# Chunks of the gate modulation loaded two ahead, in chained groups of four products; input rows loaded a pair earlier; one column's weight sums a product later

## The chip, the cores and the metric

The kernel runs on one core of one Trainium2 chip. The metric is the device time of one execution in microseconds (us), as the median over several runs. A profile of one execution shows what each engine does: TensorE (PE, with its weight loads as PEld), VectorE (DVE), ScalarE (ACT), GpSimd (POOL), and SyncE (SP), which here only issues DMAs; SPq is its queue of issues.

## The reference

One encoder layer for two sequences (prompt and sample) of 1024 rows and 1024 features, in fp32. All weights are shared.

```python
mod = jax.nn.silu(c) @ w_ada + b_ada                       # c: (1, 1024), w_ada: (1024, 6 * 1024)
sh1, sc1, ga1, sh2, sc2, ga2 = jnp.split(mod, 6)
h = rmsnorm(x, g_mix) * (1 + sc1) + sh1
z = h @ w_in                                               # latents for attention, and f_in
mix = concat(mla_group(z...), fourier_group(f_in, w_four)) @ w_out
x = x + ga1 * mix
h2 = rmsnorm(x, g_ffn) * (1 + sc2) + sh2
x = x + ga2 * ((silu(h2 @ w_gate) * (h2 @ w_up)) @ w_down)
y = rmsnorm(x, g_final)
```

## The kernel before, in words

The kernel is written in a framework that traces the Python program, orders the instructions of each engine by priority and readiness, and puts in the semaphores. So the order on an engine isn't quite that of the code; `tc.issue_after(i)` makes what is traced inside it stand behind instruction `i` on the same engine, and `behind()` (line 70) does so for the last split's two instructions. Every engine, and SP's queue of DMAs, then takes its list strictly in order.

**Products in three.** Every large fp32 product is made of three PE passes (`mm3`, lines 77 to 80): each operand is split into a rounded part and a rest by one ACT cast (line 62) and one DVE subtraction (line 63).

**Stage 1** (lines 153 to 610) works on eight pairs of row tiles, `k` = 0 to 7 (four per sequence). For a pair, `x_load` (340) loads two tiles `xt` of 128 rows into four buffers; `norm` (346) squares them on ACT, takes the root on POOL (`rstd`, 94) and scales on DVE (357); `flip` (359) transposes them on PE (370), in four groups g of two column blocks; `zproj` (397) projects one tile onto the latents and writes `lat` from DVE (418, 419) behind a root on POOL; `latents` (427) transposes `lat` on PE (433), splits it and stores both parts to `lat_d` (438); `evenodd` and `fourier_in` (381, 440) make the Fourier input, 24 passes against `wcs` each. `zproj` also stores `kv` to `ckv_d` (424). While a pair is projected the next one is flipped.

**The gate modulation** runs as filler in stage 1. `extras` (265) is a generator that `first_pair` (546) and `pair` (563) call three times a pair. It has eight chunks c of `w_ada` for the gates ga1 and ga2; a chunk is 1 MB, loaded by `mod_load` (199) as two DMAs of 512 KB, one per gate, into one of two buffers `wada`, and multiplied by `mod_mm` (207) in four products of 32 rows by 512 columns, each into its own quarter of a PSUM bank. Column groups j = 0, 1 come from the first DMA and 2, 3 from the second. At a step, the next chunk is loaded and then the present one multiplied. After the chunks, the gates' row is written out (`mod_row`, 214) and the Fourier part of `w_out` is folded with the gates (293 to 306). The shift and scale modulation earlier on (lines 465 to 529) uses the same `mod_mm`.

**The FFN** (lines 1307 to 1484, `s` the sequence) is a Strassen-like scheme over half-size blocks: 22 columns n, each of seven products `step(0)` to `step(6)` of 12 passes, into three PSUM banks x, y, z that are accumulated into more than once. Between them DVE takes sums from a bank (`u2`, 1451; `u3`, 1457, by `add`, line 137), which frees that bank for the next product into it. The weights of a column are seven combinations of four raw blocks: `sums_w` (1214) makes four differences (line 134), and `hl` (1299) splits each into two buffers `wh`, `wl`, eight of each. While column n is multiplied, the weights of n+1 are split; the sums are POOL's, but DVE makes those of the first two columns. In the first column of the first sequence (`s == 0 and n == 0`, line 1405) the last input blocks H are still being split as well (`prep`, two steps at j < 3), and the last two row tiles are transposed (`flip2`, 1239).

Of the kernel before, what the change touches and what calls it, by code (L numbers as in the profile page):

```python
# [16 lines left out]
ALU = mybir.AluOpType  # L17
# [7 lines left out]
NC = D // P  # L25
# [27 lines left out]
def hybrid_encoder_kernel(ctx: ExitStack, tc: tile.TileContext, a: dict):  # L53
    nc = tc.nc

    here = {}
# [13 lines left out]
    def behind():  # L70

        st = ExitStack()
        st.enter_context(tc.issue_after(here["a"]))
        st.enter_context(tc.issue_after(here["v"]))
        return st
# [83 lines left out]
    with ExitStack() as st:  # L159
# [36 lines left out]
        def wada_tile():  # L196
            return w2.tile([P, 4, 512], F32, tag="wada", name="wada", bufs=2)

        def mod_load(c, cols, wt):
            for j, (lo_, n) in enumerate(cols):  # L200
                nj = n // 512
                nc.sync.dma_start(
                    wt[:, j * nj : (j + 1) * nj, :],
                    a["w_ada"][c * P : (c + 1) * P, lo_ : lo_ + n].rearrange("p (j n) -> p j n", n=512))
            return wt

        def mod_mm(key, c, wt):
            if c == 0:
                mods[key] = bank()
            for j in range(4):  # L210
                here["m"] = nc.tensor.matmul(
                    mods[key][32 * j : 32 * j + 32, :], scT[:, c, :], wt[:, j, :], start=(c == 0), stop=(c == NC - 1)).ins

        def mod_row(key):
            mr = stile("modrow")
# [49 lines left out]
        def extras():  # L265


            cols1 = [(2 * D, D), (5 * D, D)]
            wt = mod_load(0, cols1, wada_tile())
            yield  # L270
            yield
            wo4 = []
            for c in range(NC):
                if c + 1 < NC:
                    nxt = mod_load(c + 1, cols1, wada_tile())
                else:
                    wo4.append(wo_load(2, wada_tile().rearrange("p a b -> p (a b)").rearrange("p (a b) -> p a b", a=2)))
                    bga = stile("bga")
                    nc.sync.dma_start(bga, a["bga"])
                mod_mm(1, c, wt)  # L280
                wt = nxt
                yield
            small_weights()
            mr = mod_row(1)
            add(mr, mr, bga, nc.vector)
            nc.sync.dma_start(ga_d, mr)
            wo4.append(wo_load(3, wada_tile().rearrange("p a b -> p (a b)").rearrange("p (a b) -> p a b", a=2)))
            yield
            for g in range(2):
                gs = slice(512 * g, 512 * g + 512)  # L290
                ga = [w.tile([P, 512], F32, tag=f"gah{s}", name="gah") for s in range(2)]
                for s in range(2):
                    nc.sync.dma_start(ga[s], ga_d[32 * g + s, :].partition_broadcast(P))
                yield
                for c in range(4):
                    k, i = c // 2, c % 2
                    ps = bank()
                    for q in range(2):
                        nc.tensor.matmul(ps[64 * q : 64 * q + 64, :], lw[:, 2 * i + q, 64 * k : 64 * k + 64], wo4[i][:, q, gs],
                                         start=True, stop=True)  # L300
                    for s in range(2):
                        so = stile("so")
                        nc.vector.tensor_tensor(out=so, in0=ps, in1=ga[s], op=ALU.mult)
                        nc.sync.dma_start(wm_d[s][:, c, gs], so)
                        if k == 1:
                            nc.sync.dma_start(
                                wn_d[NNYQ * s : NNYQ * s + NNYQ, gs].rearrange("(k r) n -> r k n", k=3)[4 * i : 4 * i + 4],
                                so[0:97:32, :].unsqueeze(1).broadcast_to([4, 3, 512]))
                    if c % 2 == 1:
                        yield  # L310
            yield
# [28 lines left out]
        def x_load(k):  # L340
            s, j = pairs[k]
            st1["x", k] = [xtile() for _ in range(2)]
            for u in range(2):
                nc.sync.dma_start(st1["x", k][u], xs[s][rows(j, u), :])
# [193 lines left out]
        with behind():  # L538
            norm(1)
        norm1 = here["p"]  # L540
        zproj(0, 0)
        evenodd(0, norm1)
        nk = len(pairs)
        more = extras()

        def first_pair():
            zproj(0, 1)
            fourier_in(0, 0)
            with tc.issue_after(here["t"]):
                flip(1, 0)  # L550
                flip(1, 1)
            next(more, None)
            latents(0, 0)
            flip(1, 2)
            flip(1, 3)
            next(more, None)
            latents(0, 1)
            next(more, None)
            fourier_in(0, 1)
            norm(2)  # L560
            evenodd(1, here["p"])

        def pair(k):
            if k == 0:
                return first_pair()
            zproj(k, 0)
            if k + 1 < nk:
                flip(k + 1, 0)
                flip(k + 1, 1)
            next(more, None)  # L570
            zproj(k, 1)
            latents(k, 0)
            here["l0"] = here["a"], here["v"]
            if k + 1 < nk:
                flip(k + 1, 2)
                flip(k + 1, 3)
            if k + 2 < nk:
                x_load(k + 2)
            next(more, None)
            fourier_in(k, 0)  # L580
            latents(k, 1)
            next(more, None)
            fourier_in(k, 1)
            if k + 2 < nk:
                norm(k + 2)
            if k + 1 < nk:
                evenodd(k + 1, here["p"])
# [559 lines left out]
    with ExitStack() as st:  # L1147
# [66 lines left out]
        def sums_w(b, out, eng):  # L1214

            b11, b21, b12, b22 = b
            t3, t2, t4 = (out(i) for i in range(3))
            sub(t3, b22, b12, eng)
            sub(b12, b12, b11, eng)
            sub(t2, b22, b12, eng)  # L1220
            here["s"] = sub(t4, b21, t2, eng)
            return [b11, t2, b21, t3, b12, t4, b22]
# [73 lines left out]
        def val():  # L1296
            return w5.tile([P, 512], F32, tag="v", name="val", bufs=VALS)
# [13 lines left out]
        for s in range(2):  # L1311
# [80 lines left out]
            for n, f in enumerate(order):  # L1392
# [10 lines left out]
                def step(j, ps, k, first, src=src):  # L1403
                    prod(ps, k, cur[j], first)
                    if s == 0 and n == 0:
                        if j == 0:
                            cur.extend(hl(v) for v in w0[4:])
                            w0.clear()
                            S["n3"] = norm3(1, S.pop("jk3").bitcast(BF16))
                        if j < 3:  # L1410
                            with behind():
                                for _ in range(2):
                                    next(prep, None)
                            if j == 1:
                                with behind():
                                    S.pop("n3")()
                            return
                        if j == 3:
                            src = S["w1"] = sums_w(src, lambda i: val(), nc.vector)
                        src = S["w1"]  # L1420
                        for i in ((), (), (), (0, 1), (2, 3), (4,), (5, 6))[j]:
                            nxt.append(hl(src[i]))
                        if j == 6:
                            flip2(3, [S.pop(("xn", 1, 3, u)) for u in range(2)], bank, lambda g: val())
                    elif s == 1 and n == 0:
                        if j == 2:
                            with tc.issue_after(here["u2"]):
                                S["w1"] = sums_w(src, lambda i: val(), nc.vector)
                        with behind(), tc.issue_after(here["c"]) if j > 1 else ExitStack():
                            for i in ((), (), (0,), (1, 2), (3,), (4,), (5, 6))[j]:  # L1430
                                nxt.append(hl(S["w1"][i]))
                        if j == 6:
                            S.pop("w1")
                    elif src is not None:
                        nxt.append(hl(src[j]))
                    if s == 0 and n == 1 and j == 2:
                        S.pop("w1", None)
# [17 lines left out]
                pend()  # L1455
                step(3, y, 6, False)
                u3 = val()
                add(u3, y, p1, nc.vector)
                step(4, z, 4, True)
                add(u3, z, u3, nc.vector)  # L1460
                pend()
# [303 lines left out]
```

## Time and profile before

| | us |
|---|---|
| median of 3 runs | 2079.11 (2078.59 to 2080.59) |
| the profiled execution, its own time | 2073.8 |
| its span | 2072.0 |
| PE busy in the span | 2023.1 |
| stage 1 (to about) | 200 |
| FFN, first column starts | 769 |

The profile is one execution; its times count from the start of its span. Rows of the timeline give start, duration, engine, line, operation, output and inputs, and in brackets the idle time ahead of it and what ended that. An fp32 product of 32 x 512 shows as two records, so a chunk's four products are x8. Rows of the table by stretches give busy time of each engine (with its number of instructions), then the granted clock of PE, the busy share of the DMA engines and GB/s. "L12" is line 12 of the kernel. PE takes up nearly the whole span, so what counts is where PE waits.

### The profile page before, as it was taken

To read this page: it belongs to the slowest core of one execution; us is meant where nothing else is said; L and a number is where in the kernel's file an instruction comes from. 1 tells how busy PE (TensorE), PEld (TensorE's weight loads), DVE (VectorE), ACT (ScalarE), POOL (GpSimd) and SP (SyncE) were. 2 spreads that over 40 slices of the span, in tenths; PEclk is the share of its full clock that TensorE was granted. 3 is DMA by queue.
4 is the path that set the end of the run, shared out by engine and by line. 5 is a ranking of instruction groups with operands and counts; after the bars stand their busy time and mean duration, and the time that the engine had idled before them with its cause. 6 is when DMAs were issued, how large, how long until landed. Compare 5 with 4: busy or idle time off the path is not lost.

```text
span 2072.0 us, 28814 instructions
## 1 busy us (share of the span) xinstructions
PE 2023.1 (98%) x10044; PEld 1659.5 (80%) x10044; DVE 1414.3 (68%) x2085; ACT 901.7 (44%) x1763; POOL 820.4 (40%) x1013
## 2 busy tenths in 40 slices
PE   6899999999999999999999999999999999999998
PEld 3688878888888877888888888877788888888886
DVE  4557767666677679767677676778665666667685
ACT  3666535555565554332333355454223232336451
POOL 0555111111313317779778510334554454420142
PEclk9999999999999999999999999999999999999999
DMA  9675885544643465546446477675322222257662
GB/s 395 216 238 180 274 316 172 134 90 102 168 102 122 154 244 203 179 157 213 173 158 219 154 274 260 212 242 182 118 102 102 96 108 102 86 171 275 230 232 94
DMA packets 185342, 375.49 MB, mean 181 GB/s; under 512 B 18764, under 2 KB 58444, under 8 KB 182124
## 3 DMA queue, kind: packets, MB, share of 16 engines
q1 hardware_dynamic: 167212, 318.06, 45.1%
q0 software_dynamic: 17984, 55.59, 9.0%
q8 instruction: 79, 1.29, 0.3%
q14 instruction: 67, 0.55, 0.1%
HBM read 259.47 MB, written 122.49 MB: 184 GB/s over the span
## 4 chain that ended last, share of the span: by engine, by line
PE 51%; DVE 4%; DMA 3%; issue 1%; ACT 1%; POOL 1%; SPq 1%; DVEq 0%; ACTq 0%; POOLq 0%
PE bank L80 17%; PE bank L79 17%; PE bank L78 17%; DVE wl L63 2%; DMA draw<-s_d 1%; DVE val L137 1%; ACT wh L62 1%; DMA H<-s_d 1%; DMA val<-x_d 1%; POOL val L137 0%; DVE val L1571 0%; DMA H<-in_w_down_dram 0%; DMA X<-hc_d 0%; SPq L1531 0%; ACT H L62 0%
## 5 line engine op out<-in xcount | busy, mean ns | idle before, releaser
L80 PE MATMUL bank<-H,wl 128*128 128x512 f32 x1232 | 491.3, 399 | 0.2 <-DVE wl L63 0.2
L78 PE MATMUL bank<-H,wh 128*128 128x512 f32 x1232 | 483.7, 393 | 2.6 <-DVE val L137 1.0
L79 PE MATMUL bank<-H,wh 128*128 128x512 f32 x1232 | 485.6, 394 | 0.3 <-DVE H L63 0.3
L79 PEld LDWEIGHTS bank<-H,wh 128*128 128x128 f32 x1232 | 231.2, 188 | 60.5 <-DVE H L63 0.6
L78 PEld LDWEIGHTS bank<-H,wh 128*128 128x128 f32 x1232 | 231.3, 188 | 59.9 <-DVE val L137 1.8
L80 PEld LDWEIGHTS bank<-H,wl 128*128 128x128 f32 x1232 | 231.3, 188 | 53.6 <-DVE wl L63 0.5
L63 DVE TENSOR_TENSOR wl<-draw,wh 128x512 fp32r<-128x512 f32 x286 | 201.6, 739 | 85.3 <-ACT wh L62 84.7
L137 DVE TENSOR_TENSOR val<-bank,val 128x512 f32<-128x512 f32 x200 | 136.6, 689 | 159.6 <-PE bank L80 152.5
L62 ACT CAST wh<-draw 128x512 fp32r<-128x512 f32 x286 | 168.7, 619 | 160.6 <-PE bank L79 81.0
L137 POOL TENSOR_TENSOR val<-val 128x512 f32<-128x512 f32 x58 | 83.2, 1444 | 367.1 <-DVE val L1545 188.6
L79 PE MATMUL bank<-wl,wh 128*128 128x512 f32 x572 | 223.7, 391 | 2.5 <-DVE wl L63 2.5
L62 ACT CAST wh<-rgu 128x512 fp32r<-128x512 f32 x172 | 106.7, 620 | 271.8 <-PE bank L79 209.4
L78 PE MATMUL bank<-wh 128*128 128x512 f32 x572 | 222.6, 389 | 0.0
L80 PE MATMUL bank<-wh,wl 128*128 128x512 f32 x572 | 222.6, 389 | 0.0
L62 ACT CAST wh<-val 128x512 fp32r<-128x512 f32 x133 | 82.1, 620 | 269.1 <-PE bank L79 256.1
L63 DVE TENSOR_TENSOR wl<-val,wh 128x512 fp32r<-128x512 f32 x133 | 132.5, 998 | 76.0 <-ACT wh L62 76.0
L63 DVE TENSOR_TENSOR wl<-rgu,wh 128x512 fp32r<-128x512 f32 x172 | 168.7, 981 | 3.6 <-ACT wh L62 3.5
L134 POOL TENSOR_TENSOR val<-rgu 128x512 f32<-128x512 f32 x80 | 116.7, 1459 | 99.5 <-DMA rgu<-in_wgu_dram 95.7
L79 PEld LDWEIGHTS bank<-wl,wh 128*128 128x128 f32 x572 | 107.3, 188 | 27.7 <-DVE wl L63 5.8
L78 PEld LDWEIGHTS bank<-wh 128*128 128x128 f32 x572 | 107.4, 188 | 22.7
L80 PEld LDWEIGHTS bank<-wh,wl 128*128 128x128 f32 x572 | 107.4, 188 | 22.0
L1024 DVE TENSOR_REDUCE mx<-ps_s 128x1 f32<-128x1024 f32 x64 | 78.2, 1222 | 62.8 <-PE ps_s L1019 62.6
(356 smaller groups left out, 4120.1 us busy)
## 6 DMA issues: line engine op xcount, KB each, us to landing
rgu<-in_wgu_dram SPq DMA_DIRECT2D x86, 512.0 KB, 4.2
draw<-s_d SPq DMA_DIRECT2D x143, 256.0 KB, 3.9
s_d<-val POOLq DMA_DIRECT2D x88, 256.0 KB, 4.2
draw<-t_d SPq DMA_DIRECT2D x88, 256.0 KB, 4.5
s_d<-val SPq DMA_DIRECT2D x66, 256.0 KB, 3.3
draw<-in_w_down_dram SPq DMA_DIRECT2D x55, 256.0 KB, 4.6
wada<-in_w_ada_dram SPq DMA_DIRECT2D x11, 1024.0 KB, 7.2
xt<-in_x_dram SPq DMA_DIRECT2D x16, 512.0 KB, 6.4
```

Of the source, the lines that this page charges most:

```text
L62: here["a"] = nc.scalar.copy(hi, src).ins
L63: here["v"] = nc.vector.tensor_tensor(out=lo, in0=src, in1=rd(hi), op=ALU.subtract).ins
L78: nc.tensor.matmul(out, lh, rh, start=first, stop=False, skip_group_check=cont)
L79: nc.tensor.matmul(out, lh, rl, start=False, stop=False, skip_group_check=cont)
L80: here["t"] = nc.tensor.matmul(out, ll, rh, start=False, stop=last, skip_group_check=cont).ins
L134: return eng.tensor_tensor(out=out, in0=x, in1=y, op=ALU.subtract).ins
L137: eng.tensor_tensor(out=out, in0=x, in1=y, op=ALU.add)
L1024: nc.vector.tensor_reduce(out=mx, in_=ps, axis=AX.X, op=ALU.max)
```

## The change

It has four parts. In `mod_mm` the four products are taken in the order j = 2, 3, 0, 1, and each stands behind the one ahead of it. In `extras` two chunks are loaded at the first step, and at each later step the present chunk is multiplied first and then the chunk two ahead loaded; the first step is moved up ahead of `zproj(0, 0)` and there is no empty step, so that the first `mod_mm` comes two calls earlier. `x_load` is called for the pair three ahead instead of two, and once more in `first_pair`. In the FFN's first column the DVE sums for the second column move from step 3 to step 4, behind `u3`, and the splits that use them with them; two more steps of `prep` come at step 3.

```diff
-            for j in range(4):
-                here["m"] = nc.tensor.matmul(
-                    mods[key][32 * j : 32 * j + 32, :], scT[:, c, :], wt[:, j, :], start=(c == 0), stop=(c == NC - 1)).ins
+            for n, j in enumerate((2, 3, 0, 1)):
+                with tc.issue_after(here["m"]) if n else ExitStack():
+                    here["m"] = nc.tensor.matmul(
+                        mods[key][32 * j : 32 * j + 32, :], scT[:, c, :], wt[:, j, :], start=(c == 0), stop=(c == NC - 1)).ins
...
-            wt = mod_load(0, cols1, wada_tile())
-            yield
+            ahead = [mod_load(c, cols1, wada_tile()) for c in range(2)]
             yield
             wo4 = []
             for c in range(NC):
-                if c + 1 < NC:
-                    nxt = mod_load(c + 1, cols1, wada_tile())
-                else:
+                mod_mm(1, c, ahead.pop(0))
+                if c + 2 < NC:
+                    ahead.append(mod_load(c + 2, cols1, wada_tile()))
+                elif c + 2 == NC:
...
-                mod_mm(1, c, wt)
-                wt = nxt
                 yield
...
+        more = extras()
+        next(more)
         zproj(0, 0)
         evenodd(0, norm1)
         nk = len(pairs)
-        more = extras()
...
             flip(1, 2)
             flip(1, 3)
+            x_load(3)
...
-            if k + 2 < nk:
-                x_load(k + 2)
+            if k + 3 < nk:
+                x_load(k + 3)
...
-                        if j < 3:
-                            with behind():
+                        if j < 4:
+                            with behind() if j < 3 else ExitStack():
                                 for _ in range(2):
                                     next(prep, None)
...
-                        if j == 3:
-                            src = S["w1"] = sums_w(src, lambda i: val(), nc.vector)
+                        if j == 4:
+                            with tc.issue_after(here["u3"]):
+                                S["w1"] = sums_w(src, lambda i: val(), nc.vector)
                         src = S["w1"]
-                        for i in ((), (), (), (0, 1), (2, 3), (4,), (5, 6))[j]:
+                        for i in ((), (), (), (), (0, 1, 2), (3, 4), (5, 6))[j]:
...
-                add(u3, y, p1, nc.vector)
+                here["u3"] = nc.vector.tensor_tensor(out=u3, in0=y, in1=p1, op=ALU.add).ins
```

What it moves on the engines is shown at three places. First PE in the first pair, from the last pass of the even Fourier product to the first of the odd one (`xt` are the flips' transposes, `lat` the latents', `wada` the chunk's products). Before:

```order
L80 MATMUL bank<-wcs_h,eol 128x280
L370 MATMUL bank<-ident,xt 128x128 x8
L433 MATMUL bank<-ident,lat 128x128 x4
L370 MATMUL bank<-ident,xt 128x128 x8
L433 MATMUL bank<-ident,lat 128x128 x4
L211 MATMUL bank<-wada,scT 32x512 x4
L78 MATMUL bank<-wcs_h,eoh 128x256
```

and now:

```order
L80 MATMUL bank<-wcs_h,eol 128x280
L369 MATMUL bank<-ident,xt 128x128 x8
L212 MATMUL bank<-wada,scT 32x512 x4
L432 MATMUL bank<-ident,lat 128x128 x4
L369 MATMUL bank<-ident,xt 128x128 x8
L212 MATMUL bank<-wada,scT 32x512 x4
L432 MATMUL bank<-ident,lat 128x128 x4
L78 MATMUL bank<-wcs_h,eoh 128x256
```

The first two chunks' groups now stand ahead of the two transposes of latents instead of one group behind both. The third chunk's group stands between the 23rd and the 24th pass of the odd Fourier product, the fourth between the 6th and 7th pass of `zproj(1, 1)`; before, the second and third stood ahead of `zproj(1, 1)` and of `fourier_in(1, 0)`.

Second SP's queue of DMAs at the same place, from the loads of pair 2 on; each `wada` number is one chunk, its x2 the two halves. Before:

```order
L344 DMA xt_456<-in_x0_dram 128x1024
L424 DMA ckv_d00_95<-kv_524 128x128
L424 DMA ckv_d01_96<-kv_524 128x128
L424 DMA ckv_d00_95<-kv_595 128x128
L424 DMA ckv_d01_96<-kv_595 128x128
L202 DMA wada_647<-in_w_ada_dram 128x1024 x2
L438 DMA lat_d00_91<-lh_655 512x1x128
L438 DMA lat_d01_92<-ll_656 512x1x128
L438 DMA lat_d00_91<-lh_684 512x1x128
L438 DMA lat_d01_92<-ll_685 512x1x128
L202 DMA wada_690<-in_w_ada_dram 128x1024 x2
```

and now, from the row behind `xt_456` on:

```order
L202 DMA wada_476<-in_w_ada_dram 128x1024 x2
L202 DMA wada_479<-in_w_ada_dram 128x1024 x2
L423 DMA ckv_d00_95<-kv_530 128x128
L423 DMA ckv_d01_96<-kv_530 128x128
L423 DMA ckv_d00_95<-kv_601 128x128
L423 DMA ckv_d01_96<-kv_601 128x128
L202 DMA wada_658<-in_w_ada_dram 128x1024 x2
L437 DMA lat_d00_91<-lh_666 512x1x128
L437 DMA lat_d01_92<-ll_667 512x1x128
L343 DMA xt_690<-in_x0_dram 128x1024
L343 DMA xt_691<-in_x0_dram 128x1024
L202 DMA wada_698<-in_w_ada_dram 128x1024 x2
```

Chunks 0 and 1 are ahead of all stores of `kv`; chunk 2 (`wada_658`) has the place of the old chunk 0; chunk 3 (`wada_698`) stands behind the store of `ll_667` and the two loads of pair 3. On DVE, `ll_667` now stands behind the two scalings of `norm(2)` (line 356), which before stood behind both `ll`; on ACT the two squares of `norm(2)` have moved ahead of `lh_666` in the same way.

Third DVE in the FFN's first column, from the last `norm3` scaling on (`H` the last input block's splits, L134 the weight sums, L137 and L1460 sums from a bank, L63 `wl` the weight splits). Before:

```order
L1232 TENSOR_SCALAR X_8646<-X_8646,rs_r 128x1024
L63 TENSOR_TENSOR H_8933<-X_8894,H_8932 128x1024
L134 TENSOR_TENSOR val<-val 128x512
L63 TENSOR_TENSOR wl<-val,wh 128x512
L63 TENSOR_TENSOR H_8933<-X_8894,H_8932 128x1024
L134 TENSOR_TENSOR val<-val 128x512 x3
L137 TENSOR_TENSOR val<-bank,val 128x512
L63 TENSOR_TENSOR wl<-val,wh 128x512 x3
L137 TENSOR_TENSOR val<-bank,val 128x512
```

and now:

```order
L1233 TENSOR_SCALAR X_8646<-X_8646,rs_r 128x1024
L63 TENSOR_TENSOR H_8933<-X_8894,H_8932 128x1024
L63 TENSOR_TENSOR wl<-val,wh 128x512
L1460 TENSOR_TENSOR val<-bank,val 128x512
L63 TENSOR_TENSOR H_8933<-X_8894,H_8932 128x1024
L134 TENSOR_TENSOR val<-val 128x512
L137 TENSOR_TENSOR val<-bank,val 128x512
L134 TENSOR_TENSOR val<-val 128x512 x2
L137 TENSOR_TENSOR val<-bank,val 128x512
L134 TENSOR_TENSOR val<-val 128x512
L63 TENSOR_TENSOR wl<-val,wh 128x512 x4
```

`u3` (L137 before, L1460 now) stands ahead of all four weight sums instead of behind them. PE's list follows: before, the 12 last transposes of `flip2` and seven passes of the second column stood between the fifth product (H4) and the sixth (H3); now the sixth and seventh follow the fifth at once, and transposes and second column come behind them. In the second column, ACT's copy of bank x (L1447 before, L1449 now) stands behind a fourth cast of weights, `wh_9161`, instead of behind the third.

## The prediction

> **What bounds the kernel now.** I read the busy time of each engine first.
>
> ```profile
> PE 2023.1 (98%) x10044; PEld 1659.5 (80%) x10044; DVE 1414.3 (68%) x2085; ACT 901.7 (44%) x1763; POOL 820.4 (40%) x1013
> ```
>
> PE is busy for 2023.1 of 2072.0 us, and the change adds and removes no product. So it can gain only where PE waits or runs at a lower clock near the moved instructions. The table by stretches, then PE's waits from 60 to 77 us, say where that is.
>
> ```profile
> 50.00:100.00 50.00, 41.11 (x252) 33.44 (x251) 30.77 (x60) 32.43 (x78) 26.59 (x54) 0.93 0.67 222
> 100.00:150.00 50.00, 50.00 (x327) 43.31 (x327) 28.53 (x56) 29.44 (x72) 26.53 (x59) 1.00 0.84 263
> ```
>
> ```profile
> PE bank L211 <- DMA wada<-in_w_ada_dram: 5.5, 1, 5.5
> PE bank L433 <- DVE lat L418: 3.4, 2, 1.8
> ```
>
> PE is idle for 8.9 us from 50 to 100 and never from 100 to 150, and the clock is 0.93 in the first stretch only. So whatever the chunks do behind 100 us, nothing is to be had there. PE's timeline shows the two kinds of wait.
>
> ```profile
> 61.77 1.03 PE L370 MATMUL bank<-ident,xt 128*128 128x128 f32 x8
> 64.63 0.63 PE L433 MATMUL bank<-ident,lat 128*128 128x128 f32 x4 [1.82 <-DVE lat L418]
> 65.10 1.04 PE L370 MATMUL bank<-ident,xt 128*128 128x128 f32 x8
> 67.69 0.63 PE L433 MATMUL bank<-ident,lat 128*128 128x128 f32 x4 [1.56 <-DVE lat L418]
> 73.83 3.12 PE L211 MATMUL bank<-wada,scT 128*32 128x512 f32 x8 [5.51 <-DMA wada<-in_w_ada_dram]
> 76.89 0.58 PE L78 MATMUL bank<-wcs_h,eoh 128*128 128x256 f32 x1
> ```
>
> Two gaps of 1.82 and 1.56 us wait for the scalings of `lat`; the next, 5.51, waits for chunk 0. Its group then takes 3.12 us, where the later ones take about 1.07:
>
> ```profile
> 85.99 1.07 PE L211 MATMUL bank<-wada,scT 128*32 128x512 f32 x8
> 99.03 0.39 PE L78 MATMUL bank<-wcs_h,eoh 128*128 128x256 f32 x1
> ```
>
> One reason is the clock, the sixth number behind the span in these rows.
>
> ```profile
> 62.00:64.00 2.00, 0.81 (x8) 0.57 (x6) 0.00 (x0) 1.25 (x5) 1.67 (x7) 1.00 0.00 0
> 70.00:71.00 1.00, 0.00 (x0) 0.00 (x0) 0.92 (x2) 1.00 (x4) 0.92 (x1) 0.96 0.92 168
> 71.00:72.00 1.00, 0.00 (x0) 0.00 (x0) 0.47 (x1) 1.00 (x4) 0.00 (x0) 0.50 1.05 254
> 76.00:78.00 2.00, 2.00 (x10) 1.12 (x7) 0.88 (x2) 1.02 (x3) 1.16 (x4) 0.57 1.17 350
> 78.00:80.00 2.00, 2.00 (x20) 2.00 (x19) 1.25 (x1) 0.00 (x0) 1.83 (x5) 1.00 0.91 256
> ```
>
> It falls to 0.50 at about 70.9, with PE idle since 68.2, and is back at about 77.7. The other reason is that the group waits in its middle for the second half of its chunk. All that chunk 0 costs here is 5.5 of waiting, 1.0 in the group and some 1.5 to 2 by the clock.
>
> **Chunks 0 and 1: both gaps are filled.** Their four DMAs now stand right behind the last input rows, which SP issues at 53.74.
>
> ```profile
> 53.74 0.84 SPq L344 DMA_DIRECT2D xt<-in_x_dram  x2
> 69.01 0.90 SPq L202 DMA_DIRECT2D wada<-in_w_ada_dram  x2
> 59.00:60.00 1.00, 1.00 (x10) 1.00 (x9) 1.00 (x1) 0.13 (x1) 0.92 (x2) 1.00 0.00 0
> ```
>
> Here the DMA share, next to last, is 0.00 from 59 to 60 and also from 62 to 64, in the row above: the DMA engines have nothing to do. 2.1 MB put there at some 350 GB/s (the row of 76 to 78) last about 6 us behind 58.7, so both chunks are in by about 65, the first by about 62. The first group stands behind the transposes that end at 62.8 and takes 1.07, to 63.9, ahead of 64.63; the second takes 66.1 to 67.2, ahead of 67.69. I cost both at nothing: the waits for `lat` cover them. With that cover gone they would cost 1.07 each.
>
> **Chunk 2: a new wait of 2 to 4 us.**
>
> ```profile
> 65.46 0.68 DVE L63 TENSOR_TENSOR eol<-eo,eoh 128x512 fp32r<-128x512 f32 x1
> 80.22 0.37 PE L78 MATMUL bank<-wz_h,hh 128*128 128x448 f32 x1
> 85.03 1.03 PE L370 MATMUL bank<-ident,xt 128*128 128x128 f32 x8
> ```
>
> With the old group gone from behind the second `lat` transposes, the odd Fourier product starts at 68.16 in place of 76.89: the last split of its input ends at 66.2. Before, its 24 passes took 3.3 us to `zproj(1, 0)` at 80.22, the first ones at low clock; at the full clock 23 of them take 2.8, and PE asks for chunk 2 at 71.0. SP issues this chunk where it issued chunk 0, at 69.01. Chunk 0 was complete at 75.0:
>
> ```profile
> 75.03 0.19 PEld L211 LDWEIGHTS bank<-wada,scT 128*32 128x32 f32 x4 [1.01 <-DMA wada<-in_w_ada_dram]
> ```
>
> So 74.9 is one end. The other is 73, if the chunk comes at once and alone: two halves of 512 KB, issued by 69.9, at 350 GB/s, because the stores of `lat` beside it come later now. The chained order of the four products, second half first, turns the wait inside the group into one ahead of it and costs nothing else: all four need both halves, and PE takes its list in order anyway. `zproj(1, 0)` follows, which took 4.8 (80.22 to 85.03), and with or without half the clock it ends between 79.5 and 83; before it ended at 85.03.
>
> **Chunk 3 sets the end.** Behind it stand the transposes of pair 2 (1.0), six passes of 0.2, and then chunk 3: PE asks for it between 81.7 and 85. The question is when it lands. SP issues it behind the store of `ll_667` and two loads of rows. `ll_667` is behind the scalings of pair 2, whose chain took this long for pair 1 and, in its last link, pair 2:
>
> ```profile
> 53.64 1.09 ACT L354 ACTIVATE junk<-xt 128x1024 bf16<-128x1024 f32 x1
> 58.64 2.41 DVE L357 TENSOR_SCALAR xt<-xt,rs_r 128x1024 f32<-128x1024 f32 x2 [2.54 <-POOL rs_r L108]
> 78.75 3.45 DVE L357 TENSOR_SCALAR xt<-xt,rs_r 128x1024 f32<-128x1024 f32 x2 [1.00 <-POOL rs_r L108]
> 70.08 0.69 DVE L63 TENSOR_TENSOR ll<-bank,lh 128x512 fp32r<-128x512 f32 x1 [0.70 <-ACT lh L62]
> ```
>
> From the first square to both scalings are 7.4 us (53.64 to 61.05), and up to 8.4 if the scalings take 3.45. ACT now squares ahead of `lh_666`, from about 69.5, so the scalings end at about 77 and `ll_667` at 77.6. Then come one store, two loads and the chunk.
>
> ```profile
> 70.80 0.56 SPq L438 DMA_DIRECT2D lat_d<-ll  x1
> 77.84 1.43 SPq L344 DMA_DIRECT2D xt<-in_x_dram  x2
> 74.71 3.09 SPq L202 DMA_DIRECT2D wada<-in_w_ada_dram  x4
> ```
>
> At about 0.5 to 0.77 us an issue the queue is through by 80.5 to 81. 0.26 + 1.05 + 1.05 = 2.36 MB move from about 79 on, at 350 GB/s for 6.7 us: chunk 3 lands at about **85.6**. (At 418 GB/s, the rate from 82 to 84 below, it would be 84; at 256, 78 to 80 above, 88.)
>
> ```profile
> 82.00:84.00 2.00, 2.00 (x11) 1.88 (x11) 1.40 (x3) 0.31 (x1) 0.00 (x0) 1.00 1.03 418
> ```
>
> So chunk 2's wait is covered: whether PE gets there at 81.7 or 85, it goes on at 85.6. The last splits `hl` of pair 1, which also stand behind these scalings on DVE now (about 80 where it was 74.9), are covered in the same way.
>
> **The sum of stage 1.** From 85.6: group 1.0, 18 passes 3.7, transposes of `lat` and of pair 2 1.4, chunk 4 1.0, even Fourier product 3.2, `lat` 0.5, chunk 5 1.0. The odd Fourier product of pair 1 starts at 97.4; before it was 99.03. And six groups are done by then instead of four, so that two groups of 1.0 are missing later on, where PE has no gap. Gain 1.6 + 2.0 = **3.6**, by a landing at 85.6; each us of landing is a us of gain, and the change breaks even at 85.6 + 3.6 = 89.2. The loads of rows for pair 3 and on change nothing on PE themselves (no wait for `xt` stands among PE's waits), but 1 MB of them is now ahead of chunk 3.
>
> **The FFN's first column.** Two waits are there.
>
> ```profile
> 788.80 0.40 PE L78 MATMUL bank<-H,wh 128*128 128x512 f32 x1
> 789.65 0.50 PE L78 MATMUL bank<-H,wh 128*128 128x512 f32 x1 [0.46 <-DVE val L137]
> 803.52 0.40 PE L80 MATMUL bank<-H,wl 128*128 128x512 f32 x1
> 804.60 0.50 PE L78 MATMUL bank<-H,wh 128*128 128x512 f32 x1 [0.68 <-DVE val L1451]
> ```
>
> ```profile
> 786.86 2.13 DVE L134 TENSOR_TENSOR val<-val 128x512 f32<-128x512 f32 x3
> 788.91 0.68 DVE L137 TENSOR_TENSOR val<-bank,val 128x512 f32<-128x512 f32 x1
> 803.87 0.68 DVE L1451 TENSOR_TENSOR val<-bank,val 128x512 f32<-128x512 f32 x1
> ```
>
> A pass starts every 0.23 us. The first wait cost 789.65 - 788.80 - 0.23 = 0.62 and is for `u3` behind four weight sums, of which the last three take 2.13; now `u3` is ahead of them: gone. The second cost 804.60 - 803.52 - 0.23 = 0.85, for `u2` behind a split. With the splits later, `u2` is earlier; late next is ACT's copy of bank x, now behind a fourth cast, which waits for a buffer that this column's fifth product frees. The trace of before doesn't show that wait: between nothing left and as much as now I take half, 0.4. Gain 1.0, between 0 (the copy later still by 0.6) and 1.5.
>
> **Sum.** 3.6 + 1.0 = 4.6, less 0.1 for the clock at chunk 3: -4.5. The profiled execution took 2073.8 and would take 2069.3; the median of the runs, 5.3 above it, goes from 2079.1 to **2074.6**. A measurement of this kernel can tell about 0.2%, 4.2 us, from no change, and the forecast lies on that bound.
>
> [...] The row of 70 to 71 shows the clock falling after 2.7 us without work. [...]
>
> **Rivals.**
> - Chunk 3 lands sooner (84 or before) and PE is there at 81.7 to 83: gain 5 to 7.5 in stage 1, 2072.5 down to 2070.5. For it: row loads and chunk move at 418 GB/s from 82 to 84. Against: its issue hangs on DVE.
> - Most is eaten: the clock halves again while PE waits for chunk 3 (2.7 us sufficed before), and one slow stretch of 3.4 us costs 1.7 (2076.3); or chunk 3 lands at 88 (2077), or the FFN gains nothing as well (2078).
> - Slower: `ll_667` comes 1 us later by the scalings of 3.45, each issue takes 0.77, and 2.36 MB from 81.3 on at 256 GB/s land at 90.5. That is 1.3 behind the break-even of 89.2; with 1.7 by the clock and nothing from the FFN it is +3, 2082.
> - It doesn't do what it says: chunks 0 and 1 land only with the stores, at 70 or later, and the first group holds up `lat` and all behind it. Against: an idle DMA queue from 59 on. It would end like the third, and shares its chance.
>
> **How the numbers follow.** Forecast 0.55, sooner 0.17, eaten 0.22, slower 0.06. The range takes in the first three: 2070.5 to 2079.5. The bound for faster is 2074.95: a bit over half the forecast's chance lies below (0.32), and all of sooner (0.17): faster 0.49. Slower, above 2083.3, has half of the last case at most: 0.03. The same: 0.48.
>
> **What would show it.** Right: a group of L212 at about 62.8 ahead of the first `lat` transposes, with no longer wait behind it; a wait of 2 to 4 us at about 71 ahead of the third group; the fourth group at about 85.6 behind a wait for its DMA; the odd Fourier product of pair 1 at about 97.4; PE without idle from 100 on. In the FFN no wait for `u3`, and 0.4 where the second product of the second column begins. Wrong: a first group behind 64, a fourth behind 89, or a wait for `hl` or `xt` in place of the chunks'.

## The result and the profile after

The changed kernel took 2082.84 us in the median of 22 runs (2079.82 to 2088.24), the kernel before 2078.16 in 22 runs beside them (2075.40 to 2082.00). The ratio is 1.0024, with a 95% interval of 1.0018 to 1.0030: slower by 5.0 us where 4.5 us less were forecast.

The two profiled executions can't be subtracted as they stand: 2072.0 and 2083.4 us of span differ by more than the medians. The timelines of PE show one reason, with the first pass of the first projection in the kernel before, in the changed one, and in an experiment (`e1_ffn`, below) that leaves everything ahead of the FFN as it was.

```profile
48.24 0.47 PE L78 MATMUL bank<-wz_h,hh 128*128 128x448 f32 x1 [0.94 <-ACT hh L62]
```

```profile
51.74 0.47 PE L78 MATMUL bank<-wz_h,hh 128*128 128x448 f32 x1 [0.55 <-ACT hh L62]
```

```profile
50.76 0.47 PE L78 MATMUL bank<-wz_h,hh 128*128 128x448 f32 x1 [0.40 <-ACT hh L62]
```

The same program reached this pass 2.5 us later in another execution. The profiled execution of before was an early one (2073.8, below the lowest of its 22 runs). So times in stage 1 are compared from this first projection on, and times in the FFN from the FFN's first pass on. From the first projection to the last Fourier pass of line 78 in stage 1 the kernel before takes 178.12 us (48.24 to 226.36); so measured, `e1_ffn` is at 178.43, and the changed kernel at 179.08.

PE's timeline of the changed kernel, the rows that answer to those of before:

```profile
66.23 1.07 PE L212 MATMUL bank<-wada,scT 128*32 128x512 f32 x8
68.13 0.63 PE L432 MATMUL bank<-ident,lat 128*128 128x128 f32 x4 [0.83 <-DVE lat L417]
69.56 1.07 PE L212 MATMUL bank<-wada,scT 128*32 128x512 f32 x8
71.19 0.63 PE L432 MATMUL bank<-ident,lat 128*128 128x128 f32 x4 [0.56 <-DVE lat L417]
77.96 1.93 PE L212 MATMUL bank<-wada,scT 128*32 128x512 f32 x8 [3.42 <-DMA wada<-in_w_ada_dram]
85.44 1.03 PE L369 MATMUL bank<-ident,xt 128*128 128x128 f32 x8
89.40 1.06 PE L212 MATMUL bank<-wada,scT 128*32 128x512 f32 x8 [1.72 <-DMA wada<-in_w_ada_dram]
101.24 0.39 PE L78 MATMUL bank<-wcs_h,eoh 128*128 128x256 f32 x1
```

Chunks 0 and 1 stand in the two gaps, which shrink from 1.82 and 1.56 to 0.83 and 0.56. Chunk 2 costs a wait of 3.42 and a group of 1.93 at half clock (0.50 from 78 to 80), chunk 3 a wait of 1.72. Taken from the first projection, chunk 3's group starts at 37.7 (37.4 forecast), and the odd Fourier product of pair 1 at 49.5 where it was at 50.8 before. Up to here the change gains 1.3 us and has two groups more behind it.

Then comes what no row of before had. PE's waits from 94 to 212 us, and their rows:

```profile
PE bank L432 <- DVE lat L417: 2.5, 4, 0.9
PE bank L432 <- POOL lat L416: 1.2, 1, 1.2
```

```profile
135.96 0.63 PE L432 MATMUL bank<-ident,lat 128*128 128x128 f32 x4 [0.35 <-DVE lat L417]
137.39 1.94 PE L298 MATMUL bank<-wada,lw 128*64 128x512 f32 x8
143.01 1.94 PE L298 MATMUL bank<-wada,lw 128*64 128x512 f32 x8
159.28 0.59 PE L432 MATMUL bank<-ident,lat 128*128 128x128 f32 x3 [0.63 <-DVE lat L417]
161.03 0.33 PE L432 MATMUL bank<-ident,lat 128*128 128x128 f32 x1 [1.17 <-POOL lat L416]
```

The transposes of `lat` wait 3.7 us there in sum, and in the kernel before 0.2. In the kernel before, the same pair 4 looked like this:

```profile
149.19 1.94 PE L299 MATMUL bank<-wada,lw 128*64 128x512 f32 x8
156.04 0.60 PE L433 MATMUL bank<-ident,lat 128*128 128x128 f32 x4
```

There a fold of `w_out` (L299, 1.94 us) stood between the projection of a tile and the transposes of its `lat`; now it is two steps earlier, in pair 3 (137.39), and the transposes are up before the scalings are done.

In the FFN, PE's waits from 770 to 860 us of the changed kernel and the row of the longest, then DVE ahead of it:

```profile
PE bank L78 <- DVE val L1453: 2.5, 1, 2.5
```

```profile
832.08 0.80 PE L78 MATMUL bank<-H,wh 128*128 128x512 f32 x1 [2.49 <-DVE val L1453]
```

```profile
824.88 3.15 DVE L1470 TENSOR_TENSOR val<-val 128x512 f32<-128x512 f32 x1
827.96 3.47 DVE L63 TENSOR_TENSOR wl<-val,wh 128x512 fp32r<-128x512 f32 x1
831.35 0.68 DVE L1453 TENSOR_TENSOR val<-bank,val 128x512 f32<-128x512 f32 x1
```

Both waits of the first two columns are gone, as forecast. But in the third column `u2` (L1453) now stands behind a split of 3.47 us, and PE waits 2.49. In the table by stretches the clock then falls for 3.4 us, from 832.0 on, to 0.51 here:

```profile
832.00:834.00 2.00, 1.92 (x5) 1.53 (x6) 2.00 (x3) 0.00 (x0) 1.70 (x2) 0.51 0.93 276
```

Matching the FFN's passes one by one with those of before, the changed kernel has lost 3.2 us by 900 us, counted from the FFN's first pass.

### The profile page after: what moved, and what is told of

Read it like the earlier page. It is cut to its first block, busy times and chain, and to the rows that moved or that the text cites. A ratio compares the mean times of both kernels' runs of the same rounds, so it can differ in the third digit from the quotient of the medians.

```text
span 2083.4 us, 28816 instructions
## 1 busy us (share of the span) xinstructions
PE 2029.7 (97%) x10044; PEld 1662.2 (80%) x10044; DVE 1412.0 (68%) x2085; ACT 901.8 (43%) x1763; POOL 820.0 (39%) x1013
## 4 chain that ended last, share of the span: by engine, by line
PE 53%; DVE 3%; DMA 2%; issue 1%; ACT 1%; POOL 1%; SPq 1%; DVEq 0%; ACTq 0%; POOLq 0%
PE bank L79 18%; PE bank L80 18%; PE bank L78 18%; DVE wl L63 1%; DMA H<-s_d 1%; DMA draw<-s_d 1%; DVE val L137 1%; ACT wh L62 1%; DVE val L1573 0%; SPq L1533 0%; SPq L1532 0%; POOL val L137 0%; DMA draw<-t_d 0%; POOL rs_y L104 0%; ACT H L62 0%
## 5 line engine op out<-in xcount | busy, mean ns | idle before, releaser
L63 DVE TENSOR_TENSOR wl<-draw,wh 128x512 fp32r<-128x512 f32 x286 | 201.0, 737 | 86.1 <-ACT wh L62 85.7
L137 POOL TENSOR_TENSOR val<-val 128x512 f32<-128x512 f32 x58 | 82.7, 1433 | 368.8 <-DVE val L1547 189.8
L63 DVE TENSOR_TENSOR wl<-val,wh 128x512 fp32r<-128x512 f32 x133 | 137.0, 1032 | 76.2 <-ACT wh L62 76.0
L137 DVE TENSOR_TENSOR val<-bank,val 128x512 f32<-128x512 f32 x156 | 106.3, 689 | 113.1 <-PE bank L80 112.9
L63 DVE TENSOR_TENSOR wl<-rgu,wh 128x512 fp32r<-128x512 f32 x172 | 166.2, 966 | 4.0 <-ACT wh L62 4.0
L134 POOL TENSOR_TENSOR val<-rgu 128x512 f32<-128x512 f32 x80 | 117.1, 1464 | 100.0 <-DMA rgu<-in_wgu_dram 96.3
```

Source lines behind the costliest of these rows:

```text
L63: here["v"] = nc.vector.tensor_tensor(out=lo, in0=src, in1=rd(hi), op=ALU.subtract).ins
L134: return eng.tensor_tensor(out=out, in0=x, in1=y, op=ALU.subtract).ins
L137: eng.tensor_tensor(out=out, in0=x, in1=y, op=ALU.add)
```

## The experiments

Each was timed beside the kernel before on the same chip. The table gives the start of the first projection, the time from there to the last Fourier pass of line 78 in stage 1 (against before's 178.12), what the FFN has lost from its first pass to the pass that before runs at 900 us, and the ratio to before.

| kernel | first projection | stage 1 | FFN to 900 | ratio, 95% interval |
|---|---|---|---|---|
| changed | 51.74 | +0.96 | +3.2 | 1.0024 (1.0018 to 1.0030) |
| `e1_ffn` | 50.76 | +0.31 | +1.8 | 1.0007 (0.9998 to 1.0016) |
| `e2_mod` | 51.63 | +1.22 | -0.1 | 1.0011 (1.0002 to 1.0019) |
| `e3_order` | 52.25 | -0.38 | +0.3 | 1.0006 (0.9998 to 1.0015) |
| `e4_ahead` | 50.75 | +1.61 | -0.7 | 1.0006 (0.9998 to 1.0015) |
| `e5_gap2` | 48.84 | -5.29 | +2.0 | 0.9982 (0.9974 to 0.9991) |
| `e5_gap1` | 51.44 | +2.38 | 0.0 | 1.0027 (1.0015 to 1.0038) |
| `e6_putnext` | 51.79 | -0.13 | -1.0 | 0.9997 (0.9988 to 1.0006) |
| `e7_u2first` | 50.62 | +0.05 | +1.2 | 1.0009 (1.0000 to 1.0017) |
| `e8_both` | 51.10 | -4.35 | -0.9 | 0.9973 (0.9962 to 0.9984) |
| `e10_xold` | 50.75 | -4.43 | -0.5 | 0.9975 (0.9966 to 0.9985) |

Between executions that are alike in a stage, stage 1 spreads by up to 0.9 us (`e5_gap2` and `e8_both` have the same one), the FFN's beginning by about 1 (more with a fall of the clock: 3.2 in the changed kernel, which has one, 1.8 in `e1_ffn`, which has none), and the start of the first projection by over 3.

Two stretches are not in the table. From stage 1's last pass to the FFN's first, the kernel before took 542.8 us, the kernels with the same stage 1 up to 544.7, and those with a moved stage 1 from 544.1 to 545.8, the changed kernel the most; whether the move costs something there, some 1 us, isn't shown. Behind 900 us all but one lose 0.2 to 4.2 us against this early execution of before, whatever their FFN is.

### The parts one by one

`e1_ffn` is the kernel before with the FFN part of the diff alone:

```diff
...
+                        if j == 4:
+                            with tc.issue_after(here["u3"]):
+                                S["w1"] = sums_w(src, lambda i: val(), nc.vector)
...
+                        for i in ((), (), (), (), (0, 1, 2), (3, 4), (5, 6))[j]:
...
```

> The kernel before with the FFN part alone. Theory F (the later splits of the second column's weights push VectorE into GpSimd's sums, so that the third column waits for u2): a wait of about 2.5 us for u2 at the third column and half clock behind it, no wait for u3 in the first column; FFN net +3, total +2 to +4 us against before. Rival N (the wait at the third column came of where the DMAs happened to fall in the one profiled execution): the FFN gains about 1 us as forecast, total -1. Stage 1 as before in both.

PE's waits from 770 to 860 us in it:

```profile
PE bank L78 <- DVE val L1452: 2.6, 1, 2.6
PE bank L78 <- ACT H L62: 0.6, 1, 0.6
```

The wait in the third column is there again, at 2.6, in another execution with another start and without the rest of the change: this speaks for theory F, and rival N is out. The clock didn't fall this time (the first two passes behind the wait took 0.50 and 0.40, where the first took 0.80 in the changed kernel), and the FFN lost 1.8 us, not 3.2.

`e2_mod` is the changed kernel without that part:

> The changed kernel without its FFN part (order of the products, chunks two ahead, rows sooner stay). Theory F with theory G (groups that are multiplied sooner are missing as filler in the later pairs, where transposes of latents then wait for their scalings): +1 to +3 us against before, with 2 to 4 us of waits for lat between 130 and 215 us; the FFN's first column as before. Rival N: the whole of the loss, +5, is here.

Stage 1 has the same waits as in the changed kernel (the two gaps at 0.83 and 0.56, chunk 2 at 3.49, chunk 3 at 1.93, and `lat` waits later), the FFN is as before, and the ratio is 1.0011. Neither part alone holds the whole loss. By the ratios only this part's loss is clear of 1.0; that of `e1_ffn` is shown by its rows.

`e3_order` has the new order and the chain in `mod_mm` alone:

> The kernel before with the order 2, 3, 0, 1 and the chain in mod_mm alone. Theory O (the products wait for the second half of each load also ahead of stage 1, where nothing else is there to do): the first projection of stage 1 starts 2 to 3.5 us later than in the profile of before (48.2), total +2 to +4. Rival D (the 3.5 us at the start are the spread of DMA times between executions): start of the first projection within 1 us of before or as far on either side, total within 1 us.

Its first projection is the latest of all, but `e6_putnext`, which has the old order, is only 0.5 earlier, and three kernels with the old order are at 50.6 to 50.8. So rival D holds in kind: the start spreads between executions, though by more than D's 1 us (4.0 here against before's profile), and no more of it can be put down to the order. From the first projection on, the order changes nothing (-0.38).

`e4_ahead` has the chunks two ahead and the rows sooner, with the old `mod_mm`:

> The kernel before with the chunks two ahead and the rows sooner, without the new order of products and without the FFN part. Theory G: waits for lat of 2 to 4 us between 130 and 215 us, which eat the gain of about 3.6 forecast at chunks 0 to 3; total within -2 to +1. The forecast's own reasoning (no gap behind 100 us): -3.6. By theory O this kernel is 2 to 4 us faster than the one with the new order as well.

Half of this was expected, half was not. The `lat` waits came (0.36 and 1.17 in pair 4, 0.69 and 0.87 in pair 6). But there was no wait for a chunk at all, and stage 1 was longer still, by 1.61. PE's groups of chunk products, by shape, from 50 to 130 us, first of this kernel and then of `e2_mod`, which has the chain:

```profile
L211 PE MATMUL bank<-wada,scT 128*32 128x512 f32 x64 | 15.8, 605 | 0.0
```

```profile
L212 PE MATMUL bank<-wada,scT 128*32 128x512 f32 x64 | 9.4, 661 | 5.4 <-DMA wada<-in_w_ada_dram 5.4
```

Each row holds the same 64 records, all eight chunks. Without the chain they keep PE busy for 15.8 us and with it for 9.4. The timeline of `e4_ahead` says why:

```profile
71.11 1.05 PE L211 MATMUL bank<-wada,scT 128*32 128x512 f32 x4
72.99 1.05 PE L211 MATMUL bank<-wada,scT 128*32 128x512 f32 x4
```

Without the chain a chunk's four products are issued as two and two, with other passes between, and each half takes 1.05 us: as long as all four together (1.07). (The order of the four differs as well; chain and order were not tried apart.) That is 6.4 us more of PE; against it stand the 5.4 us of waits for chunks 2 and 3 that `e2_mod` has and this kernel hasn't, and the two end within 0.4 us of each other in stage 1. The forecast booked the chained order at no cost and didn't see what its absence would cost.

### Is it the missing filler?

`e5_gap2` is `e2_mod` with two empty steps behind chunk 1. Chunks 0 and 1 stay in the two gaps, and each later group and each fold is back at the step where it stood before:

```diff
+                if c == 1:
+                    yield
+                    yield
```

> The kernel before with the order of products, chunks two ahead and rows sooner (no FFN part), and two empty steps behind chunk 1, so that chunks 0 and 1 fill the two first gaps and every later group and fold stands where it stood before. Theory G (the waits for lat come from missing filler): none past 30 us behind the first projection, no wait for chunks 2 and 3, first projection to the last Fourier product some 8 to 9 us shorter than before (5.5 of waiting, 2.1 of group time, 1 to 1.7 of clock), total -6 to -9. Rival E (PE is simply too early for VectorE and GpSimd, whatever stands in between): waits for lat of 2 to 4 us or for hl come up all the same, total -2 to -5.

PE's waits from 60 to 220 us:

```profile
PE bank L80 <- DVE hl L63: 1.8, 1, 1.8
PE bank L78 <- ACT hh L62: 1.5, 1, 1.5
PE bank L435 <- DVE lat L420: 1.4, 2, 0.8
```

No wait for a chunk is left, and those for `lat` are the two early gaps alone (0.79 and 0.56). Every later transposition of `lat` is 4.9 to 5.3 us earlier than before, and none waits for more than 0.14, as one did before. So PE being early does not bring these waits; taking the filler from between does. Theory G holds for `lat`. Stage 1 is 5.3 us shorter and the ratio is 0.9982: faster than before. It is 3 us less than theory G gave, and the rest stands in the first two rows: `zproj(1, 0)` waits for the splits of its own input, which stand behind the squares and the scalings of pair 2, and the clock falls behind these waits (from 79.11 on a pass of this projection takes 0.57 in place of 0.37). In the changed kernel they were under the wait for chunk 2. Waits for `hl` and a total of -2 to -5 (-3.7 measured) were signs of rival E: it is out for `lat`, but at this one place PE does come too early for ACT and DVE. The FFN's +2.0 here is one wait of 1.8 for `u3`, the one of before, and a fall of the clock behind it (0.75, 0.50 and 0.90 in the stretches of 2 us from 788 on).

`e5_gap1` has one empty step:

> The same with one empty step: every later group and fold stands one step sooner than before. Theory G: some waits for lat, 1 to 2 us in sum, and a wait for chunk 2 or none; 5 to 7 us shorter than before in stage 1. Rival E: as the kernel with two empty steps, within 1 us.

PE's waits from 60 to 260 us:

```profile
PE bank L434 <- DVE lat L419: 3.8, 4, 1.9
PE bank L434 <- POOL lat L418: 1.8, 1, 1.8
```

The two early gaps are 1.4 of these 5.6; 4.2 are later, more than in the changed kernel, where the shift is two steps. The largest stand at 190 us:

```profile
190.27 0.44 PE L434 MATMUL bank<-ident,lat 128*128 128x128 f32 x2 [1.89 <-DVE lat L419]
190.67 0.27 PE L434 MATMUL bank<-ident,lat 128*128 128x128 f32 x1
192.73 0.33 PE L434 MATMUL bank<-ident,lat 128*128 128x128 f32 x1 [1.79 <-POOL lat L418]
```

and the clock falls behind them (0.90, 0.50 and 0.75 in the stretches of 2 us from 192 on, 3.4 us at 0.50). Both theories had expected a gain here; the kernel is slower than the changed one, by +2.38 in stage 1 against +0.96. That filler decides is borne out (two steps of shift, one step, none: 3.7, 4.2, 0.1 us of late waits), that the loss falls with the shift is not: which step a piece of filler falls on matters more than by how many.

`e10_xold` is `e5_gap2` with the rows loaded two pairs ahead, as before:

> The kernel with two empty steps and without the FFN part, with the rows loaded two pairs ahead as before. If the rows sooner bring nothing of themselves (the forecast's reading) it is within 0.5 us of the kernel with two empty steps in stage 1, -3 to -5 in total. Rival X (the rows sooner set when the squares and scalings of pair 2 run, and so the waits for hl): the waits for hl of 3.3 us go, and stage 1 is 2 to 3 us shorter still.

Stage 1 is 0.86 longer than in `e5_gap2` (a `lat` wait of 0.65 has come up), but within 0.1 of `e8_both` below, which has the stage 1 of `e5_gap2`; the waits for `hh` and `hl` are the same 1.54 and 1.77, and the ratio is 0.9975. The rows sooner bring nothing that these runs can tell, as forecast, and rival X is out.

### The collision in the FFN

`e6_putnext` is `e1_ffn` with GpSimd's four sums for the stored results of the first two columns (`put_s`) behind the weight sums of the fifth column, so that GpSimd is idle, waiting for a DMA, where it had those sums:

```diff
-                if late is not None:
-                    put_s(*late)
+                if late is not None and (s, n) != (0, 2):
+                    with tc.issue_after(here["s"]) if (s, n) == (0, 3) else ExitStack():
+                        put_s(*late)
                     late = None
-                elif s == 0 and n > 0:
+                if s == 0 and n % 2:
...
```

> The kernel before with the FFN part, and the four sums on GpSimd that store the first two columns' results moved behind the weight sums of the fifth column. Theory F (the wait for u2 at the third column is a collision of VectorE's split with those very sums): the split behind the third column's u3 product takes about 0.7 instead of 3.5 us and the wait of 2.6 falls below 1; the FFN is about 1.5 us faster than with its part alone. Rival P (any GpSimd work in that place slows VectorE as much): the wait stays at 1.5 to 2.6.

DVE at that place in `e1_ffn`, then GpSimd there, then DVE in `e6_putnext`:

```profile
822.38 3.17 DVE L1469 TENSOR_TENSOR val<-val 128x512 f32<-128x512 f32 x1
825.47 3.47 DVE L63 TENSOR_TENSOR wl<-val,wh 128x512 fp32r<-128x512 f32 x1
828.86 0.68 DVE L1452 TENSOR_TENSOR val<-bank,val 128x512 f32<-128x512 f32 x1
```

```profile
823.69 1.30 POOL L137 TENSOR_TENSOR val<-val 128x512 f32<-128x512 f32 x1
825.86 2.52 POOL L134 TENSOR_TENSOR val<-val 128x512 f32<-128x512 f32 x2
```

```profile
822.87 0.68 DVE L1470 TENSOR_TENSOR val<-val 128x512 f32<-128x512 f32 x1
823.47 0.68 DVE L63 TENSOR_TENSOR wl<-val,wh 128x512 fp32r<-128x512 f32 x1
824.08 0.68 DVE L1453 TENSOR_TENSOR val<-bank,val 128x512 f32<-128x512 f32 x1
```

The same product and the same split take 0.68 each where they took 3.17 and 3.47, DVE's order being the same. PE's wait in the third column is gone; 0.2 us of one comes up in the fourth, where the moved sums now stand. The FFN is 1.0 us ahead of before's profile, where `e1_ffn` is 1.8 behind it. The collision that theory F names is shown, rival P is out for this place. In `e1_ffn` the split lasts to the end of GpSimd's two sums (828.4) and 0.6 us behind. The sum from a bank, which has one input in PSUM, took its 0.68 beside GpSimd as well, here in `e1_ffn`:

```profile
815.54 1.63 POOL L134 TENSOR_TENSOR rgu<-rgu 128x512 f32<-128x512 f32 x1
815.94 0.68 DVE L137 TENSOR_TENSOR val<-bank,val 128x512 f32<-128x512 f32 x1
```

The collision by itself is not new. In `e2_mod`, which has the old FFN, the same product, split and sums are these:

```profile
822.62 1.91 DVE L1469 TENSOR_TENSOR val<-val 128x512 f32<-128x512 f32 x1
824.45 3.51 DVE L63 TENSOR_TENSOR wl<-val,wh 128x512 fp32r<-128x512 f32 x1
824.85 2.56 POOL L134 TENSOR_TENSOR val<-val 128x512 f32<-128x512 f32 x2
```

All six experiments with the old FFN have this split at 3.5, and PE waits there for 0.1 us at most. Counted from the FFN's first pass, `u2` starts at 52.6 in `e2_mod` and at 54.7 in the changed kernel: the product starts 0.9 later and meets two GpSimd sums in place of one (3.15 for 1.91), and PE is at the place 0.8 sooner. The FFN part used up the slack that had covered the collision.

`e7_u2first` is `e1_ffn` with `u2` ahead of that split:

> The kernel before with the FFN part, and in the third column u2 ahead of the one split that stood before it on VectorE. Theory F: the wait of 2.6 is what that split takes; it goes, or 0.3 is left, and the FFN is about 1 us faster than before, as forecast. Rival P (VectorE is late as a whole): u2 waits behind the product ahead as well, and the wait is 1.5 or more, or comes back at the next column.

The wait for `u2` is gone, but PE's waits have another in its place, for `u3` of the same column:

```profile
PE bank L78 <- DVE val L1462: 2.1, 2, 1.9
```

The FFN loses 1.2 us where theory F gave a gain of about 1. Another order within DVE doesn't help where the product (3.17) and the split (2.90) together have lost 4.7 us to another engine: here rival P, which has DVE late as a whole, is nearer.

### Both together

`e8_both` is the changed kernel with the two empty steps and with `put_s` as in `e6_putnext`.

> The changed kernel with two empty steps behind chunk 1, and with the four sums on GpSimd that store the first two columns' results moved behind the weight sums of the fifth column. Theories F and G, added up: stage 1 about 5.3 us shorter than before with no wait for lat past 30 us behind the first projection, no wait above 0.5 for u2 or u3 in the first three columns of the FFN (0.5 to 1 us gained); total -4 to -7. Rival T (gains in stage 1 are lost again in what follows, by where DMAs and sums fall): total -1 to -4, with the waits in the FFN back.

It takes 2072.87 us beside 2078.41 of before, ratio 0.9973 (0.9962 to 0.9984): 5.5 us faster than before, and the changed kernel's loss is turned. This is within what theories F and G gave together (-4 to -7), and the waits in the FFN that were rival T's sign did not come back. Stage 1 is 4.35 shorter, with one late `lat` wait of 0.7, and the FFN 0.9; the waits of its first three columns are all below 1. Its interval overlaps those of `e5_gap2` and `e10_xold`, so that the FFN part is shown by its rows more than by the total.

## Why the prediction was wrong

- **Chunks 0 and 1 in the gaps:** right. Both were there in time, and the gaps hide all but little of them.
- **Chunk 2, and chunk 3 as the one that sets the end:** right. Chunk 3 at 37.7 behind the first projection, forecast 37.4; gain at the odd Fourier product 1.3, forecast 1.6. That the time came so near is in part luck: SP was through with the chunk's issues at 31.2 behind the first projection (32.3 to 32.8 forecast), and its data took 6.5 us from there (4.6 to 5.1).
- **The clock:** the wait of 1.72 for chunk 3 left it at 1.00; the second rival's half clock did not come here, and no run shows the 0.1 that the sum takes off for the clock at chunk 3. (In the kernel before the clock had fallen 2.6 us into the wait for chunk 0, where the prediction counts 2.7.)
- **"two groups of 1.0 are missing later on, where PE has no gap": this step failed, and it is the larger error in stage 1.** PE had no gap behind 100 us because groups and folds stood in front of the transposes of `lat`. The step booked two groups as saved and 0 for what they had covered. Moved by two steps, they uncover 3.7 us (0.2 before). The 3.6 us of gain in stage 1 became a loss of 1.0: of the 4.6 between, 3.5 are these waits, 0.3 the smaller gain at chunk 3, and 0.8 is left. `e2_mod` has the same 0.8, so it seems to go with the change; its cause is open. `e5_gap2`, which leaves every later group and fold at its old step, has none of these waits.
- **"So whatever the chunks do behind 100 us, nothing is to be had there"** was true of gain and overlooked loss. None of the rivals had this mechanism: each was about the landing of the chunks, or the clock and the FFN's gain. The rival "Slower" gave 2082, near the measured 2082.84, but by chunk 3 landing at 42.3 behind the first projection, where 37.7 was measured: that nearness is luck.
- **The FFN:** the two waits went, and nothing was left of the 0.4 forecast in their place. Only the wait for `u3` was the part's to remove: the one for `u2` (0.85 of the forecast) is in before's profile alone, and in none of the six experiments with the old FFN. So the -1.0 of `e6_putnext` and -0.9 of `e8_both` against that profile meet the forecast in part by luck; `e4_ahead` has -0.7 with the old FFN. **What failed is that the sum stopped at the second column.** The later splits let DVE's next product and split both meet GpSimd's sums for the stores, and PE was there sooner, which opened a wait of 2.5 in the third column: -1.0 became +1.8 without a fall of the clock, and +3.2 with one.
- **The sum:** +1.0 in stage 1 and +1.8 to +3.2 in the FFN are 2.8 to 4.2 us, beside 5.0 measured (3.7 to 6.2). What is left is within the spread of the other stretches from run to run, and isn't put down to anything.

## What to carry to other kernels

- A stretch in which an engine never waits shows that its waits are covered, not that there are none: before small work is moved out of it, look at what stands between each producer and its consumer there, and count that as the price.
- Work that fills a gap should be moved alone, with everything behind it left at its place: two empty steps made 5 us of gain out of 1 us of loss.
- Where the same VectorE instruction shows 0.7 us in one row and 3.5 in another, look for GpSimd in that time, and for the slack that hides it: a later VectorE step, or a PE that comes sooner, may lay it open.

## What the runs showed of the hardware

A chunk's products, of 32 rows into a quarter of one bank each, cost as much in twos as in fours: 1.05 us for two (`e4_ahead`), 1.07 for four that are issued back to back (the changed kernel), 15.8 (`e4_ahead`) against 9.4 us (`e2_mod`) over eight chunks.

The clock's falls, in the profiled executions of the kernel before and of the changed one, are falls to 0.50 and last 3.41 or 6.83 us, but for one at the very end of each: before from 33.4 (3.41) and 70.9 (6.83) on, in the changed kernel from 33.3 (6.83), 47.0, 77.7 and 832.0 (3.41 each) on. A short wait may or may not bring one: behind the wait of 2.5 in the changed kernel it fell, behind 2.6 at the same place in `e1_ffn` it didn't, though PE waited in both for the same instruction. In these two the wait's length doesn't tell which comes. In the 3.41 us ahead of the falls at 70.9, 77.7 and 832.0 PE was busy for 0.18, 0.08 and 0.28 of the time; a share of 0.44 (64.1 to 67.5 in the kernel before) passed without a fall. What decides it isn't shown.
